# Queueing ScalarE's weight work behind copies of sums and the norm's factor, and the closing multiplications behind the last addition

## The chip, the cores and the metric

The kernel runs on one NeuronCore of a Trainium2 chip. The engines are named as the profile names them: PE is TensorE (matmuls) with PEld for its weight loads, DVE is VectorE, ACT is ScalarE, POOL is GpSimd, and SP issues most of the transfers. Each engine works through its own list of instructions in a fixed order, and an instruction whose inputs are not there holds up everything behind it on that engine. The metric is the device time of one execution in microseconds (us); lower is better.

## The reference: what is computed

A trunk of two macaron layers works on 528 tokens (512 and 16 learned meta tokens put ahead) of width 1024. Each layer is a half-weighted feed-forward block, a mixer of gated linear attention and grouped-query attention, and a second half-weighted feed-forward block:

```
h = h + 0.5 * swiglu(rmsnorm(h, norm_gains[l, 0]), ffn_w_gate[l, 0], ffn_w_up[l, 0], ffn_w_down[l, 0])
h = h + mixer(rmsnorm(h, norm_gains[l, 1]), ...)
h = h + 0.5 * swiglu(rmsnorm(h, norm_gains[l, 2]), ffn_w_gate[l, 1], ffn_w_up[l, 1], ffn_w_down[l, 1])
```

with `swiglu(x, g, u, d) = (silu(x @ g) * (x @ u)) @ d` and `rmsnorm(x, g) = x * rsqrt(mean(x * x) + 1e-6) * g`. The hidden width is 2816. After the last layer comes `rmsnorm(h, final_norm)[:, 16:]`. All is float32.

## The kernel before

**Arithmetic.** The chip's array `h` holds the tokens with the channels on the 128 partitions, as 8 chunks of 128 channels by 528 tokens. Every weight and every operand is split into a rounded high part and a remainder, and each product is made of three matmuls (high by high, high by remainder, remainder by high). A weight tile is 128x1024: ACT casts it to its high part `whi` (L227) and DVE subtracts that from the weight to give `wlo` (L228).

**A feed-forward block.** `ffn` runs four times: layer 0 first and second (called blocks A and B here), layer 1 first and second (C and D; D works on 512 tokens, since the meta tokens are dropped). Gate and up projections go by pairs of 128-column blocks, eleven pairs in a block. For a pair the two-by-two blocks of the weight are combined by Strassen's scheme in Winograd's form, seven products instead of eight, numbered "1" to "7" in `product_of_pair` (L517 is the matmul). A product is 24 matmuls: 4 chunks of 128 channels, gate and up, 3 parts. Three tiles, X, Y and Z, take the products of a pair, and a product that goes on in X continues on what stands there: "1", "6", "7" and "4" all add to X, and between them ACT copies X out of PSUM (`snapshot`, L523). Pair 0's "7" is copied as `r`, and its "4" may not write to X before that copy is made. The products of neighbouring pairs are interleaved by `ffn_steps`: P0 1, 2; P1 1, 2; P0 6, 5; P0 7, 4, 3; P1 6, 5; P2 1; P1 7; P2 2; P1 4, 3; P2 6, 5; P3 1; P2 7; P3 2; P2 4, 3; P3 6, and so on (P1 is pair 1).

**Weights of a product.** `Weights.make` prepares tiles a fixed number of products ahead. Products "1", "2" and "4" use blocks of the weight that SP loads (`w11`, `w12`, `w22`). The other four use sums, which are made by transfers that add to what they land on, issued by POOL (L183). `sums` sets them off when "1" or "2" of a pair is made. With "1": ACT writes `s3`, the negative of `w11` (L178), POOL adds `w21` from the device's memory to it (in the profile a transfer s<-win), SP loads a second `w22`, and POOL adds `s3` to that (w<-s), which is the weight of "6", while `s3` itself is that of "7". With "2": SP loads `w21`, POOL adds `w22` to it (w<-win; the weight of "5"), ACT writes `s4`, the negative of `w12` (L178), and POOL adds the weight of "6" to that (s<-w; the weight of "3"). The tiles that are loaded to be added to come from a pool of two buffers, those written by ACT from one of three, `whi` and `wlo` from pools of four.

**The norm inside a block.** RMSnorm's factor is not multiplied into the operand. Its mean is a matmul with a constant (L399), and ACT's logarithm (L405), exponential (L376) and square (L409) with two operations on DVE make the factor `rs` from it, which is used after the products, in `hidden` (L539 on) and when the block's output is added to `h`. In A and C the squares of `h` are summed within the block (L427, L431), ahead of product "5" of pair 0; after that product `norm.rs()` is called.

**The end.** In block D the last chunks' output runs through `ending` (L1031 to L1080): by halves of 256 tokens, each chunk's product is scaled (L1045) and added to `h` (L1046), squared on ACT (L1050) and added to the sum of squares (L1052); the last chunk's square goes straight into the matmul that makes the mean (L1054). The functions `factor` and `leave` make the final norm's factor (L1059 to L1062), multiply (L1067) and send chunks to the device's memory in pairs of chunks. While the second half's chunks are made, the first half's four multiplications stand between.

**What sets the order.** A planner places every instruction when the kernel is built, on each engine's list, from the order of the code, priorities and the dependences that it knows. `tc.issue_after(x)`, in the code as `after`, makes it place what is issued inside behind instruction x on x's engine; `act` is a helper that chains functions of ACT in this manner through `prev_act` so that they stay in the written order.

Of the kernel before, what the change touches and what calls it, by code (L numbers as in the profile page):

```python
# [147 lines left out]
class Weights:  # L148

    def __init__(self, nc, raw, hi, lo, wts, win):
        self.nc, self.raw, self.hi_pool, self.lo_pool, self.wts, self.win = nc, raw, hi, lo, wts, win
        self.long = self.short = None
        self.loads = []
        for t, col in zip(PLAN, COLUMN):
            if t[0] == "op":
                self.loads.append(t[1:])
            elif col % SLAB == 0:
                self.loads.append(col // SLAB)  # L160
        self.at = {load: i for i, load in enumerate(self.loads)}
        self.made, self.fetched, self.got, self.summed, self.raws = 0, 0, {}, {}, {}
        self.pos = 0

    def dram(self, f, i, name):
        return self.win[((f[0] * 2 + f[1]) * NPAIR + i) * 4 + ("11", "12", "21", "22").index(name)]
# [45 lines left out]
            self.fetched += 1  # L212

    def make(self, upto):
        nc = self.nc
        while self.made < min(upto, len(self.loads)):
            self.fetch(self.made + 1)
            s = self.made
            load = self.loads[s]
            w = self.raws.pop(s, None)  # L220
            if w is None:
                w = self.summed.pop(load)
            hi = self.hi_pool.tile([P, SLAB], F32R, tag="whi", name=f"whi{s}")
            lo = self.lo_pool.tile([P, SLAB], F32R, tag="wlo", name=f"wlo{s}")
            for a in np.split(np.arange(SLAB), 2 if s == 0 else 1):
                cs = slice(a[0], a[-1] + 1)
                nc.scalar.copy(hi[:, cs], w[:, cs])  # L227
                nc.vector.tensor_tensor(lo[:, cs], w[:, cs], hi[:, cs].bitcast(F32), ALU.subtract)  # L228
            self.got[s] = (hi, lo)
            self.got.pop(s - 12, None)  # L230
            self.made += 1
            if not isinstance(load, int) and load[2] in "12":
                self.sums(*load, w)
# [31 lines left out]
def build(tc, ctx, xt, wts, win, par, w2, const, umask, out):  # L265
# [4 lines left out]
    def pool(name, bufs, space=None):  # L270
        if space is None:
            return ctx.enter_context(tc.tile_pool(name=name, bufs=bufs))
        return ctx.enter_context(tc.tile_pool(name=name, bufs=bufs, space=space))
# [1 line left out]
    one = pool("one", 1)  # L275
    slots = {n: pool("s_" + n, b) for n, b in dict(g=16, t=6, rs=2).items()}
    small = pool("small", 4)
    W = Weights(nc, pool("wraw", 3), pool("whi", 4), pool("wlo", 4), wts, win)
    pss = pool("pss", 2, bass.MemoryType.PSUM)

    made = [0]
# [120 lines left out]
    def rsqrt_of(acc, y, newton):  # L402

        (ms, cut), = acc.parts
        S.activation(cut(y), ms, AF.Ln, bias=eps, scale=1.0)  # L405
        act(y, y, AF.Exp, scale=-0.5)
        if newton:
            u = slot("t", n=y.shape[-1])
            S.activation(u, y, AF.Square)  # L409
            V.scalar_tensor_tensor(cut(u), ms, EPS, cut(u), ALU.add, ALU.mult)  # L410
            V.scalar_tensor_tensor(y, u, 3.0, y, ALU.subtract, ALU.mult)

# [83 lines left out]
    def ffn(l, f, norm, done, following):  # L496
# [6 lines left out]
        def product_of_pair(p, product):  # L503
# [16 lines left out]
            def snapshot(name):  # L520
                t = slots["snap"].tile([P, T], F32, tag="snap", name=nm("snap"))[:, :n]
                st[name] = v2(t)
                S.copy(st[name], acc)  # L523

            if product == "1":
                snapshot("p1")
# [54 lines left out]
        for i, step in enumerate(steps):  # L581
            if step[0] == "P":
                if step[1:] == (0, "5") and norm.acc is None:
                    for c in range(KC):
                        norm.square(c)
                product_of_pair(*step[1:])
                if step[1:] == (0, "5"):
                    rs = norm.rs()
                if i == last_op:
                    close_pools(norm.pools)  # L590
                    following()
            else:
                down(*step[1:])
# [441 lines left out]
    def ending(sums, operand, rs):  # L1035
# [5 lines left out]
        def chunk(i, c):  # L1041
            acc, w = sums[c - LATE]
            product("ffn_w_down", acc, operand, len(w), only=i, w=w)
            t, sq[i] = slot("t")[:, hs[i]], slot("t")[:, hs[i]]
            V.scalar_tensor_tensor(t, acc.half[i], -0.25, rs[:, hs[i]], ALU.mult, ALU.mult)  # L1045
            V.tensor_tensor(h(c, hs[i]), h(c, hs[i]), t, ALU.add)  # L1046
            if c == KC - 1:
                ms[i] = pair()[:, 0, : SEQ // 2]
                TE.matmul(ms[i], o1024, fin.acc[:, hs[i]], start=True, stop=False)
            S.activation(sq[i], h(c, hs[i]), AF.Square)  # L1050
            if c < KC - 1:
                V.tensor_tensor(fin.acc[:, hs[i]], fin.acc[:, hs[i]], sq[i], ALU.add)  # L1052
            else:
                TE.matmul(ms[i], o1024, sq[i], start=False, stop=True)  # L1054
            gain(c, hs[i])

        def factor(i):
            y[i], u = slot("t")[:, hs[i]], sq[i]
# [12 lines left out]
            chunk(0, c)  # L1071
        factor(0)
        chunk(1, LATE)
        leave(0, (0, 2))
        for c in range(LATE + 1, KC):
            chunk(1, c)
        leave(0, (4, 6))
        factor(1)
        leave(1, (0, 2, 4, 6))

# [98 lines left out]
```

## Time and profile before

| what | us |
|---|---|
| three runs | 2239.44, 2239.12, 2236.11 |
| their median | 2239.12 |
| the profiled execution's own time | 2237.59 |
| its span in the profile | 2235.8 |
| PE busy within it | 2197.9 (98%) |
| mean clock granted to PE | 0.998 |
| first matmul of blocks B, C and D | 782.77, 1140.6, 1877.26 |

A row of the timeline holds a start, a duration, the engine, the source line, the operation, output and input names without numbers, the tile's shape, and in square brackets how long the engine had stood idle before it and what ended that. The chain of waits is read from the rows that end last. "Landing" is when a transfer's last byte is there.

### The profile page before, as it was taken

What the parts mean: (1) busy time and instruction counts of PE and PEld (TensorE: products, weight loads), DVE (VectorE), ACT (ScalarE), POOL (GpSimd) and SP (SyncE); (2) the same over time, 40 slices, a digit from 0 to 9 for tenths busy, and PEclk for the clock granted to TensorE, in tenths of its full rate; (3) what the DMA queues carried; (4) which work ended last, traced back from release to release, by engine and by line L of the source; (5) the groups of instructions that cost most, each with busy time, mean ns of one, the idle gap of its engine ahead of it and who ended that gap; (6) DMA issues with size and microseconds to landing.
All of it is one profiled execution on the core that took longest, in us unless ns stands there. A gap on an engine that the chain in (4) does not pass through costs nothing.

```text
span 2235.8 us, 39768 instructions
## 1 busy us (share of the span) xinstructions
PE 2197.9 (98%) x16506; PEld 2093.8 (94%) x16506; DVE 1521.6 (68%) x2415; ACT 1196.6 (54%) x1769; POOL 154.1 (7%) x180
## 2 busy tenths in 40 slices
PE   7999999999999999999999999999999999999998
PEld 6999999989999999999999999999788888989897
DVE  7657567586986676565696575675878767756566
ACT  7536355454785574453575363553457836636353
POOL 1111010000000010101011110100000001101010
PEclk9999999999999999999999999999999999999999
DMA  9769563212113485866667685632121136859671
GB/s 265 211 156 225 143 170 102 84 48 77 48 39 109 127 211 156 192 179 171 176 172 199 166 215 141 176 100 76 53 80 48 48 123 167 221 150 217 161 179 66
DMA packets 88612, 315.57 MB, mean 141 GB/s; under 512 B 9840, under 2 KB 12272, under 8 KB 88432
## 3 DMA queue, kind: packets, MB, share of 16 engines
q1 hardware_dynamic: 61136, 218.26, 29.1%
q0 software_dynamic: 25344, 92.29, 23.3%
q8 instruction: 129, 2.11, 0.4%
q10 hardware_dynamic: 1952, 2.50, 0.3%
q14 instruction: 51, 0.42, 0.1%
HBM read 264.77 MB, written 2.10 MB: 119 GB/s over the span
## 4 chain that ended last, share of the span: by engine, by line
PE 86%; DVE 6%; ACT 4%; DMA 3%; issue 1%; DVEq 0%; POOL 0%; ACTq 0%; POOLq 0%
PE ss L517 37%; PE ss L393 27%; PE mm L393 13%; PE sm L393 2%; DMA w<-win 2%; DVE wlo L228 1%; PE sm L894 1%; PE ss L869 1%; ACT whi L227 1%; ACT t L376 1%; PE sm L910 1%; PE sm L911 1%; PE ss L870 1%; PE ss L399 1%; PE sm L719 0%
## 5 line engine op out<-in xcount | busy, mean ns | idle before, releaser
L517 PE MATMUL ss<-xc,whi 128*128 128x264 f32 (+1 forms) x4928 | 903.9, 285 | 16.4 <-ACT whi L227 9.5
L517 PEld LDWEIGHTS ss<-xc,whi 128*128 128x128 f32 x4928 | 767.1, 189 | 20.0 <-ACT whi L227 9.7
L517 PE MATMUL ss<-xc,wlo 128*128 128x264 f32 (+1 forms) x2464 | 702.1, 285 | 2.7 <-DVE wlo L228 2.7
L393 PE MATMUL ss<-g,whi 128*128 128x264 f32 (+2 forms) x2692 | 495.4, 300 | 0.0
L517 PEld LDWEIGHTS ss<-xc,wlo 128*128 128x128 f32 x2464 | 466.0, 189 | 5.0 <-DVE wlo L228 4.7
L393 PEld LDWEIGHTS ss<-g,whi 128*128 128x128 f32 x2692 | 391.4, 188 | 16.2
L393 PE MATMUL mm<-x,whi 128*128 128x264 f32 (+1 forms) x1712 | 384.8, 315 | 0.0
L227 ACT CAST whi<-w 128x1024 fp32r<-128x1024 f32 (+1 forms) x221 | 230.7, 1046 | 259.8 <-PE ss L393 117.0
L227 ACT CAST whi<-raw 128x1024 fp32r<-128x1024 f32 x190 | 199.3, 1049 | 293.7 <-PE mm L393 97.9
L228 DVE TENSOR_TENSOR wlo<-w,whi 128x1024 fp32r<-128x1024 f32 (+1 forms) x221 | 267.7, 1218 | 107.8 <-ACT whi L227 106.0
L393 PE MATMUL ss<-g,wlo 128*128 128x264 f32 (+2 forms) x1346 | 312.2, 300 | 0.0
L228 DVE TENSOR_TENSOR wlo<-raw,whi 128x1024 fp32r<-128x1024 f32 x190 | 232.1, 1222 | 96.1 <-ACT whi L227 94.7
L393 PEld LDWEIGHTS mm<-x,whi 128*128 128x128 f32 x1712 | 278.4, 188 | 16.6 <-issue 1.0
L393 PE MATMUL mm<-x,wlo 128*128 128x264 f32 (+1 forms) x856 | 266.1, 315 | 0.0
L393 PEld LDWEIGHTS ss<-g,wlo 128*128 128x128 f32 x1346 | 215.7, 188 | 8.3
L228 DVE TENSOR_TENSOR wlo<-s,whi 128x1024 fp32r<-128x1024 f32 x88 | 107.6, 1223 | 97.1 <-ACT whi L227 97.0
L227 ACT CAST whi<-s 128x1024 fp32r<-128x1024 f32 x88 | 92.4, 1050 | 146.7 <-PE ss L517 127.1
L393 PEld LDWEIGHTS mm<-x,wlo 128*128 128x128 f32 x856 | 159.6, 188 | 8.5 <-issue 0.7
L483 DVE SCALAR_TENSOR_TENSOR t<-ss,rs 128x528 f32<-128x528 f32 (+1 forms) x93 | 64.5, 700 | 127.1 <-PE ss L393 127.0
L178 ACT ACTIVATE s<-w 128x1024 f32<-128x1024 f32 x88 | 93.2, 1060 | 75.5 <-DMA w<-win 41.3
L183 POOL DMA_DIRECT2D w<-win x44 | 38.9, 884 | 944.5 <-DMA w<-win 430.3
L523 ACT COPY snap<-ss 128x528 f32<-128x528 f32 (+1 forms) x132 | 77.1, 584 | 0.9 <-PE ss L517 0.9
(245 smaller groups left out, 2566.8 us busy)
## 6 DMA issues: line engine op xcount, KB each, us to landing
w<-win SPq DMA_DIRECT2D x219, 512.0 KB, 4.6
raw<-wts SPq DMA_DIRECT2D x190, 512.0 KB, 3.3
s<-win POOLq DMA_DIRECT2D x44, 512.0 KB, 7.3
w<-s POOLq DMA_DIRECT2D x44, 512.0 KB, 5.5
w<-win POOLq DMA_DIRECT2D x44, 512.0 KB, 7.0
s<-w POOLq DMA_DIRECT2D x44, 512.0 KB, 7.3
h<-xt SPq DMA_DIRECT2D x3, 528.0 KB, 6.4
out<-h ACTq DMA_DIRECT2D x4, 256.0 KB, 2.3
```

Of the source, the lines that this page charges most:

```text
L178: self.nc.scalar.activation(t, w, AF.Copy, scale=-1.0)
L183: self.nc.gpsimd.dma_start(t, src, accum_op=ALU.add)
L227: nc.scalar.copy(hi[:, cs], w[:, cs])
L228: nc.vector.tensor_tensor(lo[:, cs], w[:, cs], hi[:, cs].bitcast(F32), ALU.subtract)
L376: prev_act[0] = S.activation(*args, **kw).ins
L393: TE.matmul(acc.half[i][:width], lhs, rhs[:, acc.spans[i]], start=first, stop=last)
L399: TE.matmul(a, weights, x[:, hs], start=True, stop=True)
L483: V.scalar_tensor_tensor(cut(dst[rows]), pv[rows], -0.5 * f, cut(rs[rows]), ALU.mult, ALU.mult)
L517: TE.matmul(acc[:, j], a[:, j, k], b[:, at], start=bool(begin and k == 0 and i == 0), stop=k == len(x) - 1 and i == 2, skip_group_check=no ...
L523: S.copy(st[name], acc)
L869: TE.matmul(s[:n, i, :HF], lhs, kh[:, hs], start=True, stop=False)
L870: TE.matmul(s[:n, i, :HF], lhs, kl[:, hs], start=False, stop=True)
```

## The change

`make` is renamed `make_all`, and a new `make` runs it inside `issue_after(W.behind)`, so that all of ACT's work that `make_all` issues (casts L227, negations L178) is placed behind the instruction kept in `W.behind`. That is the last `snapshot` copy while pairs 0 and 1 are worked on, the last instruction of the norm's factor on ACT right after pair 0's "5", and nothing from pair 2 on. The square in `rsqrt_of` now goes through `act`, and so stands in the chain too. In `ending`, all four multiplications of the first half, and the transfers that ACT issues for them, are placed behind the last addition of the second half. No instruction is added or taken away; SP's and POOL's lists stay in the order they had.

```diff
--- before.py
+++ after.py
@@ -149,8 +149,9 @@
 
 
 
-    def __init__(self, nc, raw, hi, lo, wts, win):
-        self.nc, self.raw, self.hi_pool, self.lo_pool, self.wts, self.win = nc, raw, hi, lo, wts, win
+    def __init__(self, tc, raw, hi, lo, wts, win):
+        nc = tc.nc
+        self.tc, self.nc, self.raw, self.hi_pool, self.lo_pool, self.wts, self.win = tc, nc, raw, hi, lo, wts, win
         self.long = self.short = None
         self.loads = []
         for t, col in zip(PLAN, COLUMN):
@@ -161,6 +162,7 @@
         self.at = {load: i for i, load in enumerate(self.loads)}
         self.made, self.fetched, self.got, self.summed, self.raws = 0, 0, {}, {}, {}
         self.pos = 0
+        self.behind = None
 
     def dram(self, f, i, name):
         return self.win[((f[0] * 2 + f[1]) * NPAIR + i) * 4 + ("11", "12", "21", "22").index(name)]
@@ -212,6 +214,10 @@
             self.fetched += 1
 
     def make(self, upto):
+        with self.tc.issue_after(self.behind) if self.behind else nullcontext():
+            self.make_all(upto)
+
+    def make_all(self, upto):
         nc = self.nc
         while self.made < min(upto, len(self.loads)):
             self.fetch(self.made + 1)
@@ -275,7 +281,7 @@
     one = pool("one", 1)
     slots = {n: pool("s_" + n, b) for n, b in dict(g=16, t=6, rs=2).items()}
     small = pool("small", 4)
-    W = Weights(nc, pool("wraw", 3), pool("whi", 4), pool("wlo", 4), wts, win)
+    W = Weights(tc, pool("wraw", 3), pool("whi", 4), pool("wlo", 4), wts, win)
     pss = pool("pss", 2, bass.MemoryType.PSUM)
 
     made = [0]
@@ -406,7 +412,7 @@
         act(y, y, AF.Exp, scale=-0.5)
         if newton:
             u = slot("t", n=y.shape[-1])
-            S.activation(u, y, AF.Square)
+            act(u, y, AF.Square)
             V.scalar_tensor_tensor(cut(u), ms, EPS, cut(u), ALU.add, ALU.mult)
             V.scalar_tensor_tensor(y, u, 3.0, y, ALU.subtract, ALU.mult)
 
@@ -520,7 +526,8 @@
             def snapshot(name):
                 t = slots["snap"].tile([P, T], F32, tag="snap", name=nm("snap"))[:, :n]
                 st[name] = v2(t)
-                S.copy(st[name], acc)
+                copied = S.copy(st[name], acc).ins
+                W.behind = copied if p < 2 else None
 
             if product == "1":
                 snapshot("p1")
@@ -586,6 +593,7 @@
                 product_of_pair(*step[1:])
                 if step[1:] == (0, "5"):
                     rs = norm.rs()
+                    W.behind = prev_act[0]
                 if i == last_op:
                     close_pools(norm.pools)
                     following()
@@ -1043,7 +1051,7 @@
             product("ffn_w_down", acc, operand, len(w), only=i, w=w)
             t, sq[i] = slot("t")[:, hs[i]], slot("t")[:, hs[i]]
             V.scalar_tensor_tensor(t, acc.half[i], -0.25, rs[:, hs[i]], ALU.mult, ALU.mult)
-            V.tensor_tensor(h(c, hs[i]), h(c, hs[i]), t, ALU.add)
+            added = V.tensor_tensor(h(c, hs[i]), h(c, hs[i]), t, ALU.add).ins
             if c == KC - 1:
                 ms[i] = pair()[:, 0, : SEQ // 2]
                 TE.matmul(ms[i], o1024, fin.acc[:, hs[i]], start=True, stop=False)
@@ -1053,6 +1061,7 @@
             else:
                 TE.matmul(ms[i], o1024, sq[i], start=False, stop=True)
             gain(c, hs[i])
+            return added
 
         def factor(i):
             y[i], u = slot("t")[:, hs[i]], sq[i]
@@ -1071,10 +1080,10 @@
             chunk(0, c)
         factor(0)
         chunk(1, LATE)
-        leave(0, (0, 2))
         for c in range(LATE + 1, KC):
-            chunk(1, c)
-        leave(0, (4, 6))
+            added = chunk(1, c)
+        with after(added):
+            leave(0, (0, 2, 4, 6))
         factor(1)
         leave(1, (0, 2, 4, 6))
 
```

In the rows that follow each engine's list is shown as it is built, by source line, operation and tile names: `w22_00_1` is block 22 of layer 0, feed-forward 0, pair 1; `whi9` the tenth weight tile's high part; `snap` a copy of X; `rs` and the `t` made from it belong to the norm's factor. The line numbers of the changed kernel are 6 to 9 higher.

Block A, ACT, the casts and the norm's factor around pair 0's "7", before:

```order
L227 CAST whi7_424<-w22_00_0_311 128x1024
L227 CAST whi8_463<-s4_00_0_171 128x1024
L227 CAST whi9_496<-w22_00_1_205 128x1024
L405 ACTIVATE rs43_452<-ss44_453,eps_88 128x528
L376 ACTIVATE rs43_452<-rs43_452 128x528
L523 COPY snap46_493<-ss25_242 128x528
L409 ACTIVATE t45_459<-rs43_452 128x528
L227 CAST whi10_536<-w21_00_1_274 128x1024
L178 ACTIVATE s3_00_2_578<-w11_00_2_467 128x1024
L227 CAST whi11_574<-w11_00_2_467 128x1024
```

And with the change:

```order
L233 CAST whi7_424<-w22_00_0_311 128x1024
L411 ACTIVATE rs43_452<-ss44_453,eps_88 128x528
L382 ACTIVATE rs43_452<-rs43_452 128x528
L529 COPY snap46_493<-ss25_242 128x528
L382 ACTIVATE t45_459<-rs43_452 128x528
L233 CAST whi8_463<-s4_00_0_171 128x1024
L233 CAST whi9_496<-w22_00_1_205 128x1024
L233 CAST whi10_536<-w21_00_1_274 128x1024
L233 CAST whi11_574<-w11_00_2_467 128x1024
L180 ACTIVATE s3_00_2_578<-w11_00_2_467 128x1024
```

The copy `snap46` (pair 0's `r`) and the factor (`rs43`, `t45`) have gone ahead of the casts `whi8` and `whi9`, and pair 2's negation `s3_00_2` now stands behind the casts `whi10`, of pair 1's sum `w21`, and `whi11`.

Block C, ACT, the place where pair 3's sums begin, before:

```order
L227 CAST whi264_13826<-s4_10_1_13396 128x1024
L523 COPY snap1081_13796<-ss1080_13757 128x528
L178 ACTIVATE s3_10_3_13937<-w11_10_3_13834 128x1024
L523 COPY snap1082_13822<-ss1056_13425 128x528
L227 CAST whi265_13830<-w22_10_2_13697 128x1024
L227 CAST whi266_13895<-w21_10_2_13762 128x1024
L227 CAST whi267_13933<-w11_10_3_13834 128x1024
```

And with the change:

```order
L529 COPY snap1081_13796<-ss1080_13757 128x528
L529 COPY snap1082_13822<-ss1056_13425 128x528
L233 CAST whi264_13826<-s4_10_1_13396 128x1024
L233 CAST whi265_13830<-w22_10_2_13697 128x1024
L233 CAST whi266_13895<-w21_10_2_13762 128x1024
L180 ACTIVATE s3_10_3_13937<-w11_10_3_13834 128x1024
L233 CAST whi267_13933<-w11_10_3_13834 128x1024
```

The negation `s3_10_3` stood ahead of the copy `snap1082` and three casts; it now stands behind both copies and behind the cast `whi266` of `w21_10_2`, a sum that a transfer makes. In block A pair 3's negation has moved in the same way.

Block D, ACT, around the copies of pair 0, before:

```order
L376 ACTIVATE rs1827_21354<-rs1827_21354 128x512
L409 ACTIVATE t1829_21360<-rs1827_21354 128x512
L227 CAST whi407_21364<-s4_11_0_21062 128x1024
L523 COPY snap1825_21323<-ss1817_21167 128x512
L178 ACTIVATE s3_11_2_21476<-w11_11_2_21368 128x1024
L227 CAST whi408_21397<-w22_11_1_21103 128x1024
L227 CAST whi409_21434<-w21_11_1_21199 128x1024
L523 COPY snap1830_21394<-ss1817_21167 128x512
L227 CAST whi410_21472<-w11_11_2_21368 128x1024
```

And with the change:

```order
L382 ACTIVATE rs1827_21354<-rs1827_21354 128x512
L529 COPY snap1825_21323<-ss1817_21167 128x512
L382 ACTIVATE t1829_21360<-rs1827_21354 128x512
L233 CAST whi406_21326<-w22_11_0_21236 128x1024
L233 CAST whi407_21364<-s4_11_0_21062 128x1024
L529 COPY snap1830_21394<-ss1817_21167 128x512
L233 CAST whi408_21397<-w22_11_1_21103 128x1024
L233 CAST whi409_21434<-w21_11_1_21199 128x1024
L180 ACTIVATE s3_11_2_21476<-w11_11_2_21368 128x1024
L233 CAST whi410_21472<-w11_11_2_21368 128x1024
```

The copies `snap1825` and `snap1830` have gone ahead, and the negation `s3_11_2` has moved behind the cast `whi409` of the sum `w21_11_1`.

The end, DVE, the first half's multiplications (L1067, and L1076 with the change) between the second half's operations, before:

```order
L1067 TENSOR_TENSOR h_82<-h_82,t1998_24603 128x2x256
L1045 SCALAR_TENSOR_TENSOR t2001_24655<-ss1989_24523,rs1827_21354 128x256
L1067 TENSOR_TENSOR h_82<-h_82,t1998_24603 128x2x256
L1046 TENSOR_TENSOR h_82<-h_82,t2001_24655 128x256
L1067 TENSOR_TENSOR h_82<-h_82,t1998_24603 128x2x256
L1045 SCALAR_TENSOR_TENSOR t2003_24680<-ss1990_24524,rs1827_21354 128x256
L1052 TENSOR_TENSOR t1978_24454<-t1978_24454,t2002_24656 128x256
L1029 TENSOR_SCALAR h_82<-h_82,par_83 128x256
L1046 TENSOR_TENSOR h_82<-h_82,t2003_24680 128x256
L1029 TENSOR_SCALAR h_82<-h_82,par_83 128x256
L1061 SCALAR_TENSOR_TENSOR t2004_24681<-ss2005_24684,t2004_24681 128x256
L1062 SCALAR_TENSOR_TENSOR t2006_24693<-t2004_24681,t2006_24693 128x256
```

And with the change:

```order
L1053 SCALAR_TENSOR_TENSOR t2001_24651<-ss1989_24523,rs1827_21354 128x256
L1054 TENSOR_TENSOR h_82<-h_82,t2001_24651 128x256
L1060 TENSOR_TENSOR t1978_24454<-t1978_24454,t2002_24652 128x256
L1037 TENSOR_SCALAR h_82<-h_82,par_83 128x256
L1053 SCALAR_TENSOR_TENSOR t2003_24676<-ss1990_24524,rs1827_21354 128x256
L1054 TENSOR_TENSOR h_82<-h_82,t2003_24676 128x256
L1076 TENSOR_TENSOR h_82<-h_82,t1998_24603 128x2x256
L1037 TENSOR_SCALAR h_82<-h_82,par_83 128x256
L1076 TENSOR_TENSOR h_82<-h_82,t1998_24603 128x2x256 x3
L1070 SCALAR_TENSOR_TENSOR t2004_24677<-ss2005_24680,t2004_24677 128x256
L1071 SCALAR_TENSOR_TENSOR t2006_24693<-t2004_24677,t2006_24693 128x256
L1076 TENSOR_TENSOR h_82<-h_82,t2006_24693 128x2x256 x4
```

The four multiplications by `t1998` now stand behind the last addition to `h` (L1046, now L1054) and ahead of the second half's factor.

## The prediction

> **What bounds the kernel now.** I read the page's first part, then the waits of PE, then the timelines of PE, ACT, POOL and DVE at those places, at last the windows for the clock.
>
> ```profile
> span 2235.8 us, 39768 instructions
> PE 2197.9 (98%) x16506; PEld 2093.8 (94%) x16506; DVE 1521.6 (68%) x2415; ACT 1196.6 (54%) x1769; POOL 154.1 (7%) x180
> PE ss L517 <- ACT whi L227: 9.5, 2, 7.3
> PE ss L517 <- ACT snap L523: 3.7, 2, 2.4
> ```
>
> PE is busy for 98% of the span and bounds the kernel; 37.9 us are idle. A change of order on ACT and DVE can win only what PE waits for, and lose whatever new waits it makes. Of the waits on ACT in products, 7.3 us are the first weight of all, which the change leaves alone; 2.2 and the two for copies (3.7) are in reach. They stand here, with the means of blocks A and C and the last chunk:
>
> ```profile
> 37.98 1.13 PE L399 MATMUL ss<-t,const 128*128 128x264 f32 x4 [1.25 <-issue]
> 42.55 0.52 PE L517 MATMUL ss<-xc,whi 128*128 128x264 f32 x2 [2.22 <-ACT whi L227]
> 44.31 0.51 PE L517 MATMUL ss<-xc,whi 128*128 128x264 f32 x2 [1.25 <-ACT snap L523]
> 1158.54 1.13 PE L399 MATMUL ss<-t,const 128*128 128x264 f32 x4 [0.66 <-DVE t L431]
> 1902.96 0.50 PE L517 MATMUL ss<-xc,whi 128*128 128x256 f32 x2 [2.44 <-ACT snap L523]
> 2225.99 0.70 PE L1049 MATMUL ss<-t,const 128*128 128x256 f32 x2 [1.75 <-DVE t L1052]
> ```
>
> The cause in A and in D is on ACT's timeline:
>
> ```profile
> 41.45 1.04 ACT L227 CAST whi<-w 128x1024 fp32r<-128x1024 f32 x1 [3.52 <-DMA w<-s]
> 42.40 0.70 ACT L405 ACTIVATE rs<-ss,eps 128x528 f32<-128x528 f32 x1
> 43.13 0.64 ACT L376 ACTIVATE rs<-rs 128x528 f32<-128x528 f32 x1
> 43.68 0.58 ACT L523 COPY snap<-ss 128x528 f32<-128x528 f32 x1
> 1901.38 1.04 ACT L227 CAST whi<-w 128x1024 fp32r<-128x1024 f32 x1 [3.74 <-DMA w<-win]
> 1902.33 0.58 ACT L523 COPY snap<-ss 128x512 f32<-128x512 f32 x1
> ```
>
> In each, a cast waits 3.5 to 3.7 us for a sum that a transfer makes, and the copy of X queued behind it, though its own input is long there, holds PE. This is what the change takes out.
>
> **Gains at the blocks' starts.** In A the factor and the copy go ahead of that cast. The copy then needs the end of "7" and the logarithm's input. PE is idle from 40.3 on (42.55 less 2.22), so "7" is done then; the mean's matmuls end at 39.1 now and stand 4 places later, and logarithm, exponential and copy take 0.70, 0.64 and 0.58 behind them: 41.1 if the mean is no later, 41.6 if it is by 0.5. DVE gets one remainder of a weight ahead of the mean's last sum, up to 1.2 us more. I take 42.05 for "4", between 41.1 and 43: 2.26 us earlier than 44.31. A second piece hangs on the clock:
>
> ```profile
> 45.00:46.00 1.00, 1.00 (x7) 0.50 1.10 225
> 49.00:50.00 1.00, 1.00 (x11) 1.00 0.93 90
> 1903.00:1904.00 1.00, 1.00 (x8) 1.00 0.68 131
> ```
>
> After A's two waits (3.5 us together, with 0.5 us of matmuls between) the granted clock fell to half: 7 matmuls in that window against 11 at full clock. It was back before 49, so 3 to 4 us at half clock, worth 1.5 to 2; I take 1.7. After D's 2.44 us alone there was no fall. With one wait of about 1.3 us A keeps its clock: another -1.7, and A starts 4.0 us earlier in all (bounds -1.3 and -5.2).
> In D the copy no longer stands behind the waiting cast, but behind the factor, which waits for the mean. In B and C the copies did not hold PE, and now stand behind the logarithm too. A copy is done 0.70 + 0.58 = 1.3 us behind the mean's end at the earliest, and "4" needs it. C's mean is placed 18 matmuls later, so that its own wait of 0.66 goes: 1.3 - 0.66, with a little for handing over, is +0.75 (0, if the mean is early enough, to 1.5). By the same reckoning D keeps 0.75 of its 2.44, so -1.7 (0 to -2.4), and B gains a wait of 0.65 (0 to 1.3).
> [...]
>
> **What is queued behind: the sums of the next pairs.** POOL's transfers of a pair start with ACT's negation, and with the change that stands behind casts of sums, themselves waiting for a transfer. What it holds up is the weight of pair 3's "6", whose cast stands ahead of pair 2's copy `r` on ACT in both orders, so PE's "4" of pair 2 waits for it in the end. The present margins:
>
> ```profile
> 75.69 0.86 POOL L183 DMA_DIRECT2D w<-s  x1 [8.58 <-DVE g L382]
> 832.72 0.87 POOL L183 DMA_DIRECT2D w<-s  x1 [8.56 <-DMA w<-win]
> 1192.06 0.89 POOL L183 DMA_DIRECT2D w<-s  x1 [9.74 <-DVE wlo L228]
> 1928.65 0.86 POOL L183 DMA_DIRECT2D w<-s  x1 [8.18 <-DMA w<-win]
> w<-s POOLq DMA_DIRECT2D x44, 512.0 KB, 5.5
> s<-win POOLq DMA_DIRECT2D x44, 512.0 KB, 7.3
> 86.66 0.41 PE L517 MATMUL ss<-xc,whi 128*128 128x264 f32 x2
> 845.75 0.41 PE L517 MATMUL ss<-xc,whi 128*128 128x264 f32 x2
> 1202.93 0.41 PE L517 MATMUL ss<-xc,whi 128*128 128x264 f32 x2
> 1941.26 0.39 PE L517 MATMUL ss<-xc,whi 128*128 128x256 f32 x2
> ```
>
> The first four rows are the transfers that finish pair 3's "6" in A, B, C and D, the last four the first matmuls of pair 2's "4". From issue it takes 5.5 us to land, then 1.05 us of cast and 0.58 of copy, 7.1 together. So "4" could start at 82.8, 839.8, 1199.2 and 1935.8, and starts 3.9, 5.9, 3.8 and 5.5 us after that: the margin of each block. Now the shift:
>
> ```profile
> 64.76 1.06 ACT L178 ACTIVATE s<-w 128x1024 f32<-128x1024 f32 x1
> 68.01 2.23 ACT L227 CAST whi<-w 128x1024 fp32r<-128x1024 f32 x2 [2.18 <-DMA w<-win]
> 1161.13 1.05 ACT L178 ACTIVATE s<-w 128x1024 f32<-128x1024 f32 x1
> 1178.99 1.06 ACT L178 ACTIVATE s<-w 128x1024 f32<-128x1024 f32 x1 [0.80 <-DVE wlo L228]
> 1184.84 2.00 ACT L227 CAST whi<-w 128x1024 fp32r<-128x1024 f32 x2 [3.36 <-DMA w<-win]
> 1895.64 1.06 ACT L178 ACTIVATE s<-w 128x1024 f32<-128x1024 f32 x1 [1.20 <-DVE wlo L228]
> ```
>
> A: pair 3's negation went at 64.76; behind the first cast of the 68.01 row it goes at about 69.0, +4.2. The blocks that SP loads for that sum take buffers which earlier products free, and those run up to 4.0 us earlier; so between +0.2 and +4.3, and I take +2.9, nearer the upper end, because the chain from one transfer to the next doesn't wait on PE. C: the negation goes from 1178.99 to about 1185.9, +6.9, and the sum it waits for is itself later, since pair 2's negation moved from 1161.13 behind two casts, +4; of that between nothing and all can be lost on the way through buffers that are not free before. So +6.9 to +10.9; I take +8.6, in the lower half, because POOL's transfer of pair 2's "6" waited for more than the negation:
>
> ```profile
> 1173.75 0.89 POOL L183 DMA_DIRECT2D w<-s  x1 [10.29 <-DVE c L550]
> ```
>
> D: pair 2's negation goes from 1895.64 to behind the cast of 1901.38 (1902.4 or later), +6.8; carried through three transfers, with some slack at each: +5.4 to +7.2, I take +6.2. B: pair 2's negation moves behind one cast of a sum as in C, +4 at most and a half of it at least as likely: +2 to +4.
> Each block then starts "4" at the later of two times, its start's gain or loss, and shift less margin. A: -4.0 against 2.9 - 3.9 = -1.0, so -1.0. B: +0.65 against at most 4 - 5.9 = -1.9, so +0.65. C: +0.75 against 8.6 - 3.8 = +4.8. D: -1.7 against 6.2 - 5.5 = +0.7. What A wins at its start is thus mostly given back some forty microseconds on.
>
> **The end.** DVE worked down the first half's multiplications between the second half's operations:
>
> ```profile
> 2224.58 0.68 DVE L1067 TENSOR_TENSOR h<-h,t 128x512 f32<-128x512 f32 x1
> 2226.11 0.42 DVE L1046 TENSOR_TENSOR h<-h,t 128x256 f32<-128x256 f32 x1
> 2228.78 0.42 DVE L1061 SCALAR_TENSOR_TENSOR t<-ss,t 128x256 f32<-128x256 f32 x1 [1.36 <-ACT t L1060]
> ```
>
> The multiplication at 2224.58 stands ahead of the last scaling; and the next multiplication but one stands ahead of the addition before it; without both the last addition goes up to 1.36 us earlier (2 x 0.68), and the factor at 2228.78 with it; the last chunk's matmuls limit that, so I take -0.9 (0 to -1.36). The four multiplications take 4 x 0.68 = 2.7 us behind the addition, where 2228.78 - 2226.53 = 2.25 us are free before the factor: up to 0.5 of the gain can go there. The first half's transfers leave later, beside the second half's work.
>
> **The sum.** -1.0 + 0.65 + 4.8 + 0.7 - 0.9 = +4.25, on the profiled execution's own 2237.59: 2241.8. C's new wait of about 4 us before "4" is as long as A's pair was, so I count one half-clock stretch, +1.7: 2243.5. Last, transfers that now start later fall among others: s<-win took 7.3 us at the median, while one that was issued in a crowd took
>
> ```profile
> s<-win POOLq DMA_DIRECT2D x1, 512.0 KB, 9.0
> ```
>
> (block D, 1897.10). Half of that excess, 0.85, in A, C and D, where the chain binds: +2.6, so 2246.1, or 2246. That is 0.31% over the median of 2239.12, which the profiled execution undercuts by 0.07%; 0.2% (4.5 us) is about what can be told from no change here, the three runs alone spread by 0.15%.
>
> **Rivals.** First, the chains are as late, but neither clock nor crowd takes its price, and some margin was larger than the rows say: 2241.8 down to no change, 2236 to 2243.6. For it: D's 2.44 us cost no clock. Second, crowding feeds on itself: in C the transfers that finish "6" of pairs 2 and 3 are issued 18.3 us apart (1173.75, 1192.06), and if PE's pairs take little longer a chain that is late stays late for several pairs, each with a wait; with 3 to 5 us more in C and A and one more half-clock stretch each, 2252 to 2262. Against it: from pair 3 on the order is the old one.
> Third, on the other side: pair 3's sum lands no later than now, because the freed buffers let SP load and POOL add earlier and the negation was never the latest input. Then the starts' gains stand: -4.0 + 0.65 + 0.75 - 1.7 - 0.9 = -5.2, 2232.4. It decides at a shift under the margins, 3.8 us in C. The POOL rows speak against it: before the transfer at 1192.06 POOL was idle 9.74 us, waiting for the transfer that follows the negation.
> [...]
> Fourth, the new order leaves PE's waits as they are and only the end gains: 2236.7.
>
> **How the numbers follow.** The forecast's own case, 2243.6 to 2252, has 0.42; the first rival 0.30, the second 0.16, the third 0.10, the fourth 0.02. Slower by over 0.2% is above 2243.6: 0.42 + 0.16 = 0.58. Within 0.2%: 0.30 + 0.02 = 0.32. Faster: 0.10. The range of 2235 to 2256 leaves out the third rival and half of the second, 0.18. The likeliest case's own range is 2243.6 to 2252.
>
> **What would show it.** Right: in A PE starts pair 0's "4" at about 42, with the clock at 1.00 from 45 to 46; in D the 2.44 us wait is under 1; PE waits in C for ACT's copy some 60 us into the block, about 4 to 5 us, and POOL's transfer for pair 3's "6" is issued 8 us later than now, measured from the block's start; that wait is the largest of the changed kernel after the first weight. DVE's first half multiplications stand in one row behind L1054. Wrong: no wait of PE at pair 2's "4" in C (third rival), or waits that return in pairs 3 to 6 (second).

## The result, and the profile after

The changed kernel takes 2250.97 us (median of six runs, 2246.75 to 2255.0) against 2239.34 us for the kernel before (six runs beside them, 2236.11 to 2242.48). The ratio is 1.0052, with a 95% interval of 1.0037 to 1.0068: slower, by about half a per cent. The profiled execution of the changed kernel is one of its longer ones, 2254.25 us of its own with a span of 2252.5; what follows explains those 16.7 us of span, of which the median keeps 11.6.

The first part of the page after, and what PE waits for:

```profile
span 2252.5 us, 39748 instructions
PE 2204.3 (98%) x16506; PEld 2099.1 (93%) x16506; DVE 1521.1 (68%) x2415; ACT 1194.8 (53%) x1769; POOL 154.6 (7%) x180
PE ss L523 <- ACT snap L529: 14.9, 7, 5.1
PE ss L523 <- ACT whi L233: 9.0, 2, 7.4
```

The waits for copies were to go and have grown from 3.7 us to 14.9. PE's idle time went up by 10.3 us (37.9 to 48.2), and its busy time by 6.4 us with the same number of matmuls: that is clock, granted at 0.994 in the mean against 0.998 before. PE's timeline has these waits over 0.6 us behind ACT that the change made or moved:

```profile
41.84 0.51 PE L523 MATMUL ss<-xc,whi 128*128 128x264 f32 x2 [1.22 <-ACT snap L529]
70.03 0.51 PE L523 MATMUL ss<-xc,whi 128*128 128x264 f32 x2 [1.60 <-ACT whi L233]
91.65 0.81 PE L523 MATMUL ss<-xc,whi 128*128 128x264 f32 x2 [4.32 <-ACT snap L529]
812.26 0.51 PE L523 MATMUL ss<-xc,whi 128*128 128x264 f32 x2 [0.69 <-ACT snap L529]
1170.48 0.51 PE L523 MATMUL ss<-xc,whi 128*128 128x264 f32 x2 [1.04 <-ACT snap L529]
1217.40 0.81 PE L523 MATMUL ss<-xc,whi 128*128 128x264 f32 x2 [5.08 <-ACT snap L529]
1915.41 0.51 PE L523 MATMUL ss<-xc,whi 128*128 128x256 f32 x2 [0.68 <-ACT snap L529]
1957.28 0.50 PE L523 MATMUL ss<-xc,whi 128*128 128x256 f32 x2 [1.90 <-ACT snap L529]
2243.38 0.70 PE L1062 MATMUL ss<-t,const 128*128 128x256 f32 x2 [0.97 <-ACT t L1058]
```

At 41.84 stands pair 0's "4" in A, which was at 44.31. At 91.65, 1217.40 and 1957.28 stands pair 2's "4" in A, C and D, where nothing waited before. The row at 70.03 is pair 2's "6" in A. The first matmuls of blocks B, C and D and the last mean, before and after, give a ledger:

```profile
782.77 0.39 PE L517 MATMUL ss<-xc,wlo 128*128 128x264 f32 x1 [0.47 <-DVE wlo L228]
1140.60 0.51 PE L517 MATMUL ss<-xc,whi 128*128 128x264 f32 x2 [0.75 <-DVE t L483]
1877.26 0.38 PE L517 MATMUL ss<-xc,wlo 128*128 128x256 f32 x1 [0.53 <-DVE wlo L228]
2227.09 0.70 PE L1054 MATMUL ss<-t,const 128*128 128x256 f32 x2 [0.41 <-ACT t L1050]
```

```profile
790.05 0.39 PE L523 MATMUL ss<-xc,wlo 128*128 128x264 f32 x1 [0.47 <-DVE wlo L234]
1148.30 0.51 PE L523 MATMUL ss<-xc,whi 128*128 128x264 f32 x2 [0.84 <-DVE t L489]
1893.40 0.38 PE L523 MATMUL ss<-xc,wlo 128*128 128x256 f32 x1 [0.53 <-DVE wlo L234]
```

A and the mixer behind it lose 7.3 us (790.05 less 782.77), B 0.4, C and its mixer 8.4, and D up to the last mean 0.15, in which 1.4 us of gain at the end are already counted. Behind that mean the end is 0.4 us longer (span less row: 8.7 and 9.1). With each matmul's start set against the start of the same matmul before, A is 3.75 us ahead at 60 us and 6.5 behind at 130; D gains 2.2 at its start and returns 3.7 at pair 2's "4".

POOL's timeline shows how late the sums are: pair 3's transfer for "6" in A, C and D. (L183 and L178, ahead of the new `make`, became L185 and L180, 2 higher and not 6 to 9.)

```profile
82.90 0.86 POOL L185 DMA_DIRECT2D w<-s  x1 [8.07 <-DMA w<-win]
1208.52 0.89 POOL L185 DMA_DIRECT2D w<-s  x1 [8.06 <-DMA w<-win]
1949.77 0.86 POOL L185 DMA_DIRECT2D w<-s  x1 [7.51 <-DMA s<-win]
```

Counted from each block's first matmul, those in C and D went from 51.5 to 60.2 and from 51.4 to 56.4 us; A's, from 75.69 to 82.90. PE's "4" starts 8.8, 8.9 and 7.5 us after these rows: landing, cast and copy (in A 7.1, 1.04 and 0.59 us).

### The profile page after: what moved, and what is told of

The parts are those of the page before. It is cut to its first block, busy times and chain, and to the rows that moved or that the text cites. A ratio compares the mean times of both kernels' runs of the same rounds, so it can differ in the third digit from the quotient of the medians.

```text
span 2252.5 us, 39748 instructions
## 1 busy us (share of the span) xinstructions
PE 2204.3 (98%) x16506; PEld 2099.1 (93%) x16506; DVE 1521.1 (68%) x2415; ACT 1194.8 (53%) x1769; POOL 154.6 (7%) x180
## 4 chain that ended last, share of the span: by engine, by line
PE 82%; DVE 6%; DMA 5%; ACT 4%; issue 2%; SPq 0%; POOL 0%; DVEq 0%; POOLq 0%; ACTq 0%
PE ss L523 33%; PE ss L399 26%; PE mm L399 13%; DMA w<-win 3%; PE sm L399 2%; DMA s<-win 2%; DVE wlo L234 1%; PE sm L902 1%; DMA w<-s 1%; PE ss L877 1%; PE sm L918 1%; ACT whi L233 1%; PE sm L919 1%; PE ss L405 1%; PE ss L878 1%
## 5 line engine op out<-in xcount | busy, mean ns | idle before, releaser
L523 PE MATMUL ss<-xc,whi 128*128 128x264 f32 (+1 forms) x4928 | 909.1, 286 | 27.2 <-ACT snap L529 14.9
L180 ACT ACTIVATE s<-w 128x1024 f32<-128x1024 f32 x88 | 93.2, 1060 | 70.0 <-DMA w<-win 38.9
L185 POOL DMA_DIRECT2D w<-win x44 | 40.1, 911 | 939.7 <-DVE wlo L234 416.4
L529 ACT COPY snap<-ss 128x528 f32<-128x528 f32 (+1 forms) x132 | 77.2, 585 | 16.7 <-PE ss L523 16.7
```

What stands on the lines that cost most here:

```text
L180: self.nc.scalar.activation(t, w, AF.Copy, scale=-1.0)
L185: self.nc.gpsimd.dma_start(t, src, accum_op=ALU.add)
L523: TE.matmul(acc[:, j], a[:, j, k], b[:, at], start=bool(begin and k == 0 and i == 0), stop=k == len(x) - 1 and i == 2, skip_group_check=no ...
L529: copied = S.copy(st[name], acc).ins
```

## The experiments

**Negations early.** The changed kernel, and the negations of pairs 2 and 3 made one step ahead of both sums' casts:

```diff
...
+            first = None
+            if not isinstance(load, int) and load[2] == "6" and load[1] in (1, 2):
+                self.fetch(s + 3)
+                f, i, name = self.loads[s + 2]
+                t = self.long.tile([P, SLAB], F32, tag="wsa", name=f"s3_{f[0]}{f[1]}_{i}")
+                first = nc.scalar.activation(t, self.raws[s + 2], AF.Copy, scale=-1.0).ins
+                self.early[f, i] = t
...
-                nc.scalar.copy(hi[:, cs], w[:, cs])
+                with self.tc.issue_after(first) if first else nullcontext():
+                    nc.scalar.copy(hi[:, cs], w[:, cs])
```

> The changed kernel, with one thing more: pair 2's and pair 3's negation (s3) is made ahead of the casts of the two sums of the pair before (w22 and w21), still behind the copies. Theory, late negations are what the change loses by: the transfers of pair 3's sum start as early as before the change or earlier, the waits of PE at pair 2's "4" in A (4.3 us), C (5.1) and D (1.9) and the one of 1.6 us at pair 2's "6" in A go, with the half-clock stretches behind them; the starts' gains stay. 2231 to 2236. Rival, the casts of weights that now stand behind copies and the norm's factor are late by themselves: the waits stay at half or more, 2244 to 2251.

It took 2236.69 us (2234.25 to 2238.04), ratio to the kernel before 0.9982 (0.9971 to 0.9992), about 14 us under the changed kernel. The four late waits are gone, as the theory says. The total is just over its range, mostly because A, 3.2 us ahead at its start, kept only 0.9: PE now waits there for a cast and its remainder that the planner put behind a load of ACT's table (1.28 us in the trace of the change). A half-clock step in the mixer behind A, at the place that the last section shows, took another 1.3 us.

```profile
52.48 0.50 PE L534 MATMUL ss<-xc,whi 128*128 128x264 f32 x2 [0.70 <-ACT whi L244]
53.74 0.39 PE L534 MATMUL ss<-xc,wlo 128*128 128x264 f32 x1 [0.76 <-DVE wlo L245]
1162.94 0.51 PE L534 MATMUL ss<-xc,whi 128*128 128x264 f32 x2 [1.04 <-ACT snap L540]
```

The wait at C's start stays at 1.04 us: that is the price of the copy behind the logarithm.

**Negations late.** The kernel before, with the two negations behind `cast5`, which is the last cast made for a product "5", so of a sum w21:

```diff
...
-            s3 = self.negative(f, i, "s3", w)
+            with self.tc.issue_after(self.cast5) if i in (2, 3) else nullcontext():
+                s3 = self.negative(f, i, "s3", w)
```

> The kernel before, with one thing changed: pair 2's and pair 3's negation is queued behind the cast of the sum w21 of the pair before; casts, copies, the norm's factor and the end stay as they were. Theory, late negations: the waits at pair 2's "4" appear in C (2 to 5 us) and in A (0 to 4) with a clock fall each, while the old waits at the starts stay, 2244 to 2253. Rival, the casts' own lateness: no new waits, 2237 to 2242.

2249.62 us (2247.55 to 2253.22), ratio 1.0036 (1.0023 to 1.0049). The total is in the theory's range, the places are not: C had no new wait, A one of 0.70, and the large ones came in B and D, and there at pair 1's "4".

```profile
818.34 0.88 POOL L185 DMA_DIRECT2D w<-win  x1 [9.24 <-DVE wlo L231]
818.99 1.12 POOL L185 DMA_DIRECT2D w<-s  x1
831.92 0.81 PE L522 MATMUL ss<-xc,whi 128*128 128x264 f32 x2 [5.83 <-ACT snap L528]
```

In these two blocks the planner, given the late negation, had also turned POOL's list round and put pair 2's transfer for w21 ahead of the one that finishes w22. So the run did two things, and its total could not settle the question; it was repeated with POOL's list held (`finished` is the transfer that finishes w22):

```diff
...
-            self.add(s1, self.dram(f, i, "22"))
+            with self.tc.issue_after(self.finished) if i == 2 else nullcontext():
+                self.add(s1, self.dram(f, i, "22"))
```

> As the second experiment (the kernel before, pair 2's and pair 3's negation behind the cast of w21), with POOL's list held to the order of the kernel before, in which pair 2's transfer for w22 goes ahead of that for w21. Theory one, the late negation alone takes the margin: new waits at pair 2's "4" in C, B or D of 2 us and more, 2246 to 2253. Theory two, the lateness must add up from pair 1 on, and two late negations stay within the margins of 3.8 to 5.9 us: no wait over 1 us at pair 2's "4", 2238 to 2243.

2251.36 us (2247.28 to 2258.21), ratio 1.0051 (1.0032 to 1.007), in the range of theory one. The profiled execution is the fastest of its five and has the wait in C; A had none, D's old one stayed, and B had one of 2.26 us near its start.

```profile
1199.06 0.89 POOL L185 DMA_DIRECT2D w<-s  x1 [7.80 <-DMA w<-win]
1208.92 0.81 PE L523 MATMUL ss<-xc,whi 128*128 128x264 f32 x2 [3.40 <-ACT snap L529]
```

By the median, late negations alone thus cost about as much as the whole change. The trace doesn't put all of that down to them: of the 9.6 us that its last mean comes later than before, the wait in C and its clock fall make 6.2. B's wait near its start and its clock fall make 3.4, and a wait of 1.20 us stood at that place in the run with the end alone, too, where nothing in B's lists had moved. And C had no such wait in the second experiment, although all engines' lists are the same in C in the two runs: there the transfer that finishes pair 3's "6" took 4.5 us, here 8.2.

**The two sums' transfers exchanged.** The changed kernel, with POOL's transfers for pairs 2 and 3 in the other order:

```diff
...
-            self.add(s2, s3)
+            self.late = (s2, s3) if i in (2, 3) else None
+            if not self.late:
+                self.add(s2, s3)
...
-            self.add(s1, self.dram(f, i, "22"))
+            first = self.add(s1, self.dram(f, i, "22"))
+            if self.late:
+                with self.tc.issue_after(first):
+                    self.add(*self.late)
```

> The changed kernel, with POOL's transfers for w21's sum of pairs 2 and 3 issued ahead of the one that finishes w22's, not 0.6 us behind it. Theory, crowding makes half of the loss (the two transfers that add to tiles share their time): the one that finishes w22 goes from 7.1 to 8.8 us back to 5 to 6, and w21's sum lands some 10 us earlier, so that the negations behind its cast go earlier too; the waits at pair 2's "4" fall by 2 to 4 us each, 2238 to 2245. Rival, the transfers' length is set by the other traffic and w21's sum isn't what the negation waits for last: 2247 to 2253.

2287.74 us (2284.0 to 2289.82), ratio 1.0204 (1.0181 to 1.0227): outside both ranges, on the far side. w21's sum could not go 10 us earlier, since its base is loaded only about when the negation's sum lands; so both transfers still ran together, and w22's took longer: 10.4 and 11.3 us for pairs 2 and 3 in A, against 8.8 and 7.1. PE waits at pair 2's "4" in all four blocks, in A:

```profile
96.92 0.81 PE L528 MATMUL ss<-xc,whi 128*128 128x264 f32 x2 [8.42 <-ACT snap L534]
```

Which of the two goes first matters by itself: the chain runs through w22. This is also what the large waits in B and D of the second experiment were: its repetition differs from it in four places of POOL's list alone, two in B and two in D, and there those waits are gone.

**Only the factor.** The changed kernel with `W.behind` set by the norm's factor and not by copies:

```diff
-                W.behind = copied if p < 2 else None
+                if W.behind and p >= 2:
+                    W.behind = None
```

> The changed kernel without the part that queues weights' work behind the copies: only the norm's factor (behind which casts and negations stand after pair 0's "5") and the end remain. Pair 3's negation then stands ahead of the cast of w21, as before the change, and only pair 2's is behind it, in A and C. Theory, late negations: A keeps its gain of some 4 us at the start, the waits at pair 2's "4" are under 2 us, 2233 to 2240. Rival, the factor's place itself costs the time: 2244 to 2251.

2243.52 us (2241.19 to 2247.74), ratio 1.0016 (1.0005 to 1.0027): between the two ranges, so neither forecast held. A gains 4.7 us at its start and then loses 8.8 in one place:

```profile
68.74 0.81 PE L523 MATMUL ss<-xc,whi 128*128 128x264 f32 x2 [6.77 <-ACT snap L529]
```

This is pair 1's "4": its copy stands behind the cast of pair 2's "6", whose sum is late through pair 2's negation. The mechanism is the one expected of pair 3, one pair earlier, where I had not looked for it. C has only 1.1 us at its start.

**Only the copies.** The changed kernel without the line behind the factor:

```diff
-                    W.behind = prev_act[0]
```

> The changed kernel without the line that queues weights' work behind the norm's factor; copies and end stay. Pair 3's negation stands behind the cast of w21 in all four blocks, pair 2's in B, C and D. Theory, late negations: A and C still wait 2 to 5 us at pair 2's "4", 2244 to 2252. Rival, the factor's place is what loses: 2233 to 2240.

2248.28 us (2243.27 to 2252.51), ratio 1.0038 (1.0023 to 1.0053), as the theory says; waits at pair 2's "4" of 4.82 us in A, 3.96 in D, and in C:

```profile
1212.88 0.81 PE L523 MATMUL ss<-xc,whi 128*128 128x264 f32 x2 [3.69 <-ACT snap L529]
```

Factor alone costs about 4 us, copies alone about 10, both 11.6. The intervals (1 to 6, 5 to 12 and 8 to 15 us) are too wide to say whether the parts add up.

This run also sizes what pair 2's negation does in A, since it keeps its place there while pair 3's has moved:

```profile
80.04 0.86 POOL L185 DMA_DIRECT2D w<-s  x1 [7.92 <-DMA w<-win]
88.79 0.81 PE L523 MATMUL ss<-xc,whi 128*128 128x264 f32 x2 [4.82 <-ACT snap L529]
```

Pair 3's "6" is issued 4.2 us later than before, counted from the block's first matmul, and A ends 3.6 us behind. With the whole change it was 7.1 us, and 6.5 behind.

**The first copies free.** The changed kernel, with nothing behind the copy of product "1":

```diff
-                W.behind = copied if p < 2 else None
+                W.behind = copied if p < 2 and name != "p1" else None
```

> The changed kernel, but nothing is queued behind the first copy of pairs 0 and 1 (the one behind product "1"); the other copies, the factor and the end as changed. Theory two: in B, C and D pair 1's sum w22 lands some 18 us after the block's first matmul, as before the change, and not 22; pair 3's lands 3 to 4 us earlier than with the change, and C's wait of 5.1 us falls to 1 to 2.5; A stays as with the change, since its pair 1 was not late: 2243 to 2248. Theory one, pair 3's negation behind the cast decides alone: C waits 4 to 5 us as before, 2248 to 2253.

2242.99 us (2241.03 to 2252.5), ratio 1.0012 (1.0001 to 1.0024): at the lower edge of theory two's range and far from theory one's, although pair 3's negation stands behind the cast all the same. (The kernel before took 2241.08 us beside these runs, so the ratio says more than the time.) Pair 1's sum w22 lands 18.2 us after C's first matmul, as theory two says, against 18.2 before and 22.3 with the change. C's new wait is gone altogether, A's "4" waits 2.65 us and B has a new one:

```profile
853.60 0.51 PE L523 MATMUL ss<-xc,whi 128*128 128x264 f32 x2 [3.05 <-ACT snap L529]
```

Block C in one table, us after the block's first matmul, from POOL's and PE's timelines (w<-s finishes "6", s<-win follows the negation):

| kernel | pair 1 w<-s | pair 2 s<-win | pair 3 s<-win | pair 3 w<-s | pair 2 "4" |
|---|---|---|---|---|---|
| before | 11.9 | 22.0 | 40.5 | 51.5 | 62.3 |
| changed | 14.4 | 28.8 | 51.3 | 60.2 | 69.1 |
| negations early | 13.7 | 26.9 | 45.1 | 54.7 | 63.9 |
| negations late, held | 11.7 | 24.4 | 47.7 | 56.3 | 66.2 |
| first copies free | 11.7 | 25.9 | 47.1 | 54.6 | 63.7 |

The lateness adds up from pair to pair: 2.5, 6.8, 10.8 us with the change. The first part of it is no negation: by the lists, the casts of pair 1's "2" and pair 0's "6" go behind the copy of product "1", and the buffer of that "6" is what SP's next load for a sum waits for: in C it is issued 7.6 us after the block's first matmul before, 10.3 with the change and 7.6 with the first copies free. Taking out that part, or the negations' part, kept the shift at pair 3's w<-s to 3.1 or 3.2 us in the one trace of each, under the margin of 3.8.

**The end alone.** The part of the change in `ending`, and the square of the norm's factor in ACT's chain, but no queueing of weights' work:

> Only the change to the end: the first half's four multiplications behind the last addition. By the tails of the other runs the last matmul to the end is 1.4 us shorter, and nothing else moves: 2237 to 2239, within the noise of before. Rival, the later transfers of the first half cost what the earlier factor gains: the last matmul comes 0.5 us earlier and the end not at all.

2238.09 us (2236.16 to 2239.97), ratio 0.9996 (0.9987 to 1.0005): not to be told from before. In its trace, as in all with this part, the last mean comes 1.4 us earlier against the matmuls ahead of it, and the factor's first operation waits for the four multiplications. From that mean to the end it takes 9.2 us against 8.7 before, longer and not 1.4 us shorter as expected, so 0.9 of the 1.4 is left:

```profile
2229.25 1.89 DVE L1074 TENSOR_TENSOR h<-h,t 128x512 f32<-128x512 f32 x3
2231.05 0.42 DVE L1068 SCALAR_TENSOR_TENSOR t<-ss,t 128x256 f32<-128x256 f32 x1
```

**A version that beats both.** The queueing only in blocks A and D, where it took a wait away, with the negations early there; B and C as before (`l == f` holds in A and D alone); the end as changed:

```diff
...
+EARLY_NEGATION = (((0, 0), 1, "5"), ((0, 0), 2, "6"), ((1, 1), 1, "6"), ((1, 1), 2, "6"))
...
-                W.behind = copied if p < 2 else None
+                W.behind = copied if p < 2 and l == f else None
...
-                    W.behind = prev_act[0]
+                    W.behind = prev_act[0] if l == f else None
```

> The changed kernel, with its queueing kept to blocks A and D, where PE waited before, and with the negations there made early: A's of pair 2 ahead of the cast of w21, A's of pair 3 and D's of pairs 2 and 3 ahead of the casts of both sums; B and C as before the change, and the end as changed. Theory, late negations cost and the copies' places gain: A keeps 2.5 to 4 us, D about 2, the end 1.4, B and C nothing, so 6 to 7 us under before, 2232 to 2235. Rival, what the copies gain is given back by the casts behind them whatever the negations do: 2236 to 2240.

2232.89 us (2231.22 to 2235.12), ratio 0.9976 (0.9967 to 0.9985), within the theory's range. A keeps 2.9 us, D 2.5, the last mean 1.4, while B, whose lists are as before, loses 1.2; the clock never falls between its start and its end:

```profile
42.18 0.51 PE L536 MATMUL ss<-xc,whi 128*128 128x264 f32 x2 [1.22 <-ACT snap L542]
1897.20 0.51 PE L536 MATMUL ss<-xc,whi 128*128 128x256 f32 x2 [0.68 <-ACT snap L542]
```

## Why the prediction was right, and where its terms were not

The direction and the mechanism were right: late negations make late sums, and PE waits at pair 2's "4" forty to fifty us behind the place that was changed. The time lies in the likeliest case's own range, 5 us above the forecast (2246 forecast, 2250.97 measured). It does so with one block's term wrong and two others right in part by luck. Term by term, in the profiled executions, where the whole is +16.7 us and not +11.6:

- **A's start**, -4.0 forecast: "4" starts at 41.84, 2.5 us earlier, without a fall of the clock (1.00 from 40.26 to 50.50); 3.75 us ahead by 60 us. Right.
- **A's return**, forecast as a shift of +2.9, so -1.0 net and 0.85 for crowding. Measured +6.5 net; the shift of pair 3's "6" from issue to issue is 7.2 (7.1 counted from the block's first matmul). This is the term that failed. The step that moved pair 3's negation by +4.2 and credited it with what PE's earlier start frees had left out that pair 2's negation, too, moves in A, behind one more cast. On ACT's timeline, pair 2's negation before, then pair 2's and pair 3's after:

```profile
46.04 1.05 ACT L178 ACTIVATE s<-w 128x1024 f32<-128x1024 f32 x1
48.27 1.06 ACT L180 ACTIVATE s<-w 128x1024 f32<-128x1024 f32 x1
72.50 1.05 ACT L180 ACTIVATE s<-w 128x1024 f32<-128x1024 f32 x1
```

  Pair 3's stood at 64.76. The first 2.2 us (1.0 for the cast, the rest from w21's sum, which landed later), with two transfers that took 9.8 and 8.8 us and not 7.5 and 5.8, made pair 2's "6" wait (70.03) and pair 3's negation 7.7 us late. With pair 2's negation in its place, in the run with the copies only, the shift was 4.2: the forecast's +4.2 without the 1.3 that the freed buffers were to give back. So, by these single traces, pair 2 makes some 3 us of the 7.1. Why the transfers took longer in A stays open.
- **B**, +0.65: +0.4 measured, but by luck. The shift was put at 2 to 4 us and is 5.7, just under the margin of 5.9.
- **C**, +0.75 at the start and +4.8 net, with 1.7 of clock and 0.85 of crowding 7.35 in all: +1.4 at the start and 8.4 to 8.6 in all. The place, the wait (5.08) and its clock fall came as described; the shift was 8.7 from issue to issue against 8.6. Of its making only a part was named: the early casts behind the copy of "1", which the experiment with the first copies free showed, were not in the sum. And the transfer that follows pair 3's negation landed 10.2 us later, of which slack took up 1.4: the row at 1192.06, which the prediction read as a wait for that transfer, names DVE's `wlo`, and the transfer had landed at 1189.93.
- **D**, -1.7 and +0.7 net with 0.85: the wait at the copy went from 2.44 to 0.68, 2.2 us gained, 3.7 returned; +1.5 against +1.55. The sum is right in part by luck: 1.6 of the 3.7 is a clock fall that the forecast did not have in D.
- **The end**, -0.9: 1.4 at the last mean, less 0.4 behind it. Right, and the half microsecond of multiplications that could stick out did.
- **Clock**, one fall in C: there were falls in A (two, at 70.98 and 91.46), C (one, at 1214.44, of double length, 6.83 us) and D (at 1958.55), besides one in a mixer (at 579.56). PE's busy time rose by 6.4 us, where the sum had 1.7 won in A and 1.7 lost in C, so nothing.

The first rival (chain late, but without price of clock or crowd) fell with the clock falls in A, C and D; the third, that the chain would be hidden, fell with the waits at pair 2's "4". The second, that a late chain stays late for several pairs, did not come: from pair 3 on no wait returned. The fourth, that only the end gains, fell with the waits that went and came in A, C and D.

## What to carry to other kernels

An instruction that waits at the head of an in-order queue is not moved back for nothing: look at all that moves back with it, and follow that work through every queue to the next time the bottleneck engine needs it, here forty to fifty us on. Cheap instructions that start a long chain (here a negation of 1.05 us, or a cast of 1.04 us that frees a buffer) belong ahead of those that wait for a transfer, and a reordering is best kept to the places where a trace showed the wait.

## What the runs showed of the hardware

**Waits and the granted clock.** In the traces before and after, PE's granted clock changes at multiples of 3.41 us: it stood at half for 3.41 us at a time, once (C, from 1214.44) for 6.83. Windows of PE cut at these multiples, columns us, busy (matmuls), clock, DMA share and GB/s: D before the change, whose wait of 2.44 us lies across two of them, then D after it, whose 1.90 us lie in one.

```profile
1898.14:1901.55 3.41, 2.20 (x17) 1.00 1.07 211
1901.55:1904.96 3.41, 2.00 (x16) 1.00 0.81 150
1904.96:1908.37 3.41, 3.41 (x31) 1.00 0.75 294
```

```profile
1955.14:1958.55 3.41, 1.51 (x13) 1.00 1.06 290
1958.55:1961.96 3.41, 3.41 (x18) 0.50 1.06 256
```

Start and end of the kernel aside, five such windows at full clock in these two traces had 1.90 to 3.41 us of idle time (2.51 at 41.29 before; 2.03 at 67.57, 3.41 at 88.05, 2.13 at 1211.03 and 1.90 at 1955.14 after), and half clock followed each. The others had at most 1.41 us (1901.55 before), and full clock followed, but for the one at 576.15 below. In the experiment with the first copies free, after waits of 2.65 us at 89.51 and 3.05 at 853.60, matmuls went on 0.12 us apart, as at full clock. So a longer wait did not always cost more: D's 1.90 us were followed by 3.41 us at half clock, worth 1.7 us of PE's work, and its 2.44 us before the change by none. Whether a wait's place among these windows decides this was not tried by a run of its own. The changed kernel's mean clock was 0.994 to 0.996 over its six runs, with 0.998 in the profiled execution before, and that may be part of why its times spread.

**A half-clock step without idle time.** In the mixer of layer 0 the clock fell for 3.41 us after the change, with no idle time ahead. The trace with the first copies free has such a step there too, from about 575.8; those before, of the end alone and of the late negations held have none. After the change:

```profile
576.27 1.03 PE L841 MATMUL ss<-const,t 128*128 128x2 f32 x8
576.15:579.56 3.41, 3.41 (x31) 1.00 0.00 0
579.56:582.97 3.41, 3.41 (x18) 0.50 0.01 2
```

At this place twenty matmuls of 2 or 16 columns, 0.11 us apart, stand within 2.6 us. After the change all twenty lie in the window ahead of the fall; before, 6 lie in one window and 14 in the next, and full clock (1.00) followed both. Whether these matmuls make the clock fall was not tried by a run of its own.

**The same transfer took 4.5 to 8.2 us.** The transfer that finishes pair 3's "6" in C took 5.0 us before, 7.2 with the change, 4.5 in the second experiment and 8.2 in its repetition, whose lists are the same on all engines in that block. Why was not shown. These 3.7 us between the last two are about as much as C's margin of 3.8, so that one profile of such a chain shows where it breaks, not how often.
